# A chunked delta-rule kernel: 32x32 block inverses on VectorE become 16x16, and TensorE does the merging

## The chip, the cores and the metric

One core of one Trainium2 chip runs the whole program. The metric is device microseconds of one execution, the median of several runs. Engine names are short: PE is TensorE's matmul and PEld its weight load, DVE is VectorE, ACT is ScalarE, POOL is GpSimd, SP is SyncE, whose queue here issues almost all DMAs.

## The reference, cut to what matters

The reference is a two-layer backbone over 512 latent and 256 context tokens of width 1024. Layer 0 has window attention beside a bidirectional RWKV-7 mixer, layer 1 a Fourier mixer, and both have a squared-ReLU MLP. The change touches the RWKV scan alone, which the reference writes as a recurrence over tokens, once forward and once backward, for 8 heads of 64:

```python
def step(S, inp):
    r_t, w_t, k_t, v_t, kk_t, a_t = inp
    s_kk = jnp.einsum('bhvk,bhk->bhv', S, kk_t)
    S = (S * w_t[:, :, None, :]
         - s_kk[..., None] * (kk_t * a_t)[:, :, None, :]
         + v_t[..., None] * k_t[:, :, None, :])
    return S, jnp.einsum('bhvk,bhk->bhv', S, r_t)
```

## The kernel before, in words

The kernel takes the tokens in chunks of 64. Within a chunk the recurrence is a triangular system: a 64x64 matrix with ones on its diagonal has to be inverted for each head, chunk and direction. Two chunks make a window of 128 tokens, and there are six windows (two of context, four of latent tokens). So `inverse(i)` inverts, for window `i`, 16 systems in each of two directions. They lie in the tiles `AB[d]` (`ab` in the trace, one of them `sB`), with the rows of a matrix on the partitions.

The work of a window runs through named pieces, which the string `PLAN` (line 1735) lists: `prep` builds decayed keys (`L`, `pgth`, `gq`, `pr`), `mats` makes the matrices on PE and masks them on DVE (`ab`, `ed`), `nat` transposes keys, `inv` is `inverse`, and `u`, `s`, `y` are the serial chain: right-hand side and solution (`zs`, `vu`), the next state (`St`), the output (`y`). `u` of a window needs its inverse and the state that the window before left. Beside them stand the projections (`tile`, dense 128x512 matmuls `ps<-hhi,whi` and the like), attention (`qry`, `max`, `row`, `attn`, with `pT` and `q`), and after them `read` and `out`. Everything behind (both MLPs, the Fourier layer) needs what these give.

`PLAN` is not the order of execution. Every instruction is recorded first (class `Plan`, line 238), and `solve` (line 382) sorts them by engine: a list scheduler with a cost per instruction (`cost`, line 336), a priority from the longest way to the end, buffers as resources, and a guess of TensorE's clock, so that it sets extra matmuls (`warm`, line 646) into gaps that it foresees. `issue` (line 613) then writes the program, so that every instruction shows line 656 and is told apart by its tiles. On each engine the order is fixed: an instruction that waits holds up all behind it.

`inverse` (line 1218) before the change has three parts:

- Gather (lines 1229 to 1250): the 32x32 diagonal blocks go to DRAM (`Dg`) and come back with one block on each of 128 partitions, in the tiles `Minv` and `Mt`. A block takes two partitions, one for each half of 16 rows. Five copies on ACT turn blocks round. `Minv` and `Mt` fill both buffers of the pool tag `p4`.
- VectorE (lines 1252 to 1299): the inverse of each 16x16 half is built by doubling, from 2x2 to 4x4, 8x8 and 16x16, in the tile `Rt`. Then the 16x16 halves are merged to 32x32: four products and four sums over 128x1024 elements (lines 1288 to 1294), with copies on ACT around them, the last a transposition of 64x1024.
- Merging on PE (lines 1301 to 1325): the inverse goes through DRAM (`D2`, `D3`, `D` in the trace) back into `ab` and `Xs`, rows on the partitions. Two groups of 32 small matmuls (32x32 by 32 columns), with an eviction behind each, merge 32x32 blocks to 64x64.

Of the kernel before, what the change touches and what calls it, by code (L numbers as in the profile page):

```python
# [50 lines left out]
def _cst_layout():  # L51
    n = 0
    for name, w in (
        ("ident", 128), ("cent", 128), ("perm", 128), ("mAB", 128), ("mED", 128),
        ("blk", 128), ("hind", 2), ("ones", 1), ("onez", 1), ("sel", 2), ("scan", 512),
        ("cos", T), ("sin", T), ("mS", 384),
    ):
        _CST[name] = (n, n + w)
        n += w
# [6 lines left out]
def _consts():  # L66
# [22 lines left out]
    put("onez", (p > 0)[:, None])  # L89
    put("sel", np.stack([p % 32 == 0, p % 32 == 1], 1))  # L90
# [574 lines left out]
def body(tc, I, out):  # L665
# [547 lines left out]
    I2 = ()  # L1213
    Rt = P.tile([128, 1024], F32, name="Rt")
    pool.memset(Rt, 0.0)
    pool.memset(sub(Rt, 0, [[33, 32]]), 1.0)

    def inverse(i):
        o = O[i]
        ABf = [o.AB[d].rearrange("p c h e t -> p (c h e) t") for d in range(2)]  # L1220
        if i in I2:
            M, Mb, tt = h2("E", name="Minv"), h2("E", name="Mb"), sB
        else:
            Mp, tt = p4((128, 1024), "Minv"), p4((128, 1024), "Mt")
            M, Mb = Mp[:, 0:512], Mp[:, 512:1024]
        Mt = tt
        Dg = dr.tile([2, 2, 16, 1024], F32, tag="Dg", bufs=2, name="Dg")
        rows = lambda u, d: slice(64 * u + 32 * d, 64 * u + 32 * d + 32)
        for d in (1, 0):
            qo = 64 if d == 0 else 0  # L1230
            for b in range(2):
                nc.sync.dma_start(Dg[d, b].rearrange("p (i t) -> i p t", t=32), ABf[d][qo + 32 * b : qo + 32 * b + 32, :, 32 * b : 32 * b + 32])
            Df = Dg[d].rearrange("b p e -> (b p) e")
            for u in range(2):
                if d:
                    nc.sync.dma_start(Mt[rows(u, d), :], Df)
                else:
                    nc.sync.dma_start(M[rows(u, d), :], Df[:, 0:512])
            if d == 0:
                nc.sync.dma_start(Mt[rows(1, 0), 0:496], Df[:, 528:1024])  # L1240
# [4 lines left out]
        by_row, by_col = [[32, 16], [1, 16]], [[1, 16], [32, 16]]  # L1245
        for u in range(2):
            r = rows(u, 1)
            act.copy(part(M, r, 0, by_row), part(Mt, r, 528 * u, by_col))
            act.copy(part(M, r, 16, by_row), part(Mt, r, 512, by_col))
        act.copy(part(M, rows(1, 0), 0, by_row), part(Mt, rows(1, 0), 0, by_row))  # L1250
        R = Rt
# [860 lines left out]
```

## Time and profile before

| | |
|---|---|
| median of 3 runs | 1432.41 us (1432.25 to 1432.7) |
| the profiled execution's own time | 1429.67 us |
| its span, first to last instruction | 1427.9 us |
| PE, DVE, ACT busy over the span | 94%, 60%, 47% |
| mean granted TensorE clock | 0.949 |
| the six inverses, from the first `Dg` issue to the last `D` issue | 202.9 to 504.1 us |

The busy share of PE is not its share of useful work: matmuls are pipelined, their ends are modelled, and at half the granted clock the same matmul is busy for longer. So PE's busy time is read together with the granted clock of the same stretch.

### The profile page before, as it was taken

The numbers are of one execution on the slowest core, as the hardware profiler recorded it, in microseconds if no ns is written. First come the engines' busy times: TensorE is split into PE (matmuls) and PEld (weight loads), VectorE is DVE, ScalarE is ACT, GpSimd is POOL, SyncE is SP. The second block draws the span as 40 slices with busy tenths as digits, with TensorE's granted clock in tenths as the row PEclk, the third lists the DMA queues.
The fourth block names the chain that finished last, engine by engine and source line by source line (L and its number), as shares of the span: only waits on it lengthen the run. The fifth ranks groups of instructions, "written<-read, shape, count | busy, mean of one in ns | idle before, by whom it ended". The sixth has DMA issues, their size and how long they took to land.

```text
span 1427.9 us, 23855 instructions
## 1 busy us (share of the span) xinstructions
PE 1337.8 (94%) x8865; PEld 1083.8 (76%) x8865; DVE 850.9 (60%) x1540; ACT 671.9 (47%) x1331; POOL 328.8 (23%) x352
## 2 busy tenths in 40 slices
PE   6999987788988999999999999999989999999997
PEld 2787875676865776887888888878967888888886
DVE  3844489997585753778655566675976333333334
ACT  3775677664454324446522255332646522255332
POOL 1436476334344233040000000000561000000001
PEclk9999998855799999999999999999999999999999
DMA  9468975736545322335555565562322232323222
GB/s 359 158 214 255 317 230 152 198 97 159 164 132 154 90 71 82 96 89 167 194 178 182 178 193 185 188 211 81 104 59 82 95 97 89 97 95 103 89 89 74
DMA packets 166148, 208.76 MB, mean 146 GB/s; under 512 B 45000, under 2 KB 78792, under 8 KB 166032
## 3 DMA queue, kind: packets, MB, share of 16 engines
q1 hardware_dynamic: 164144, 205.30, 46.8%
q10 hardware_dynamic: 1376, 1.90, 0.4%
q8 instruction: 69, 1.13, 0.3%
q14 instruction: 47, 0.39, 0.1%
q0 software_dynamic: 512, 0.03, 0.0%
HBM read 180.15 MB, written 27.00 MB: 145 GB/s over the span
## 4 chain that ended last, share of the span: by engine, by line
PE 57%; DVE 3%; DMA 1%; issue 1%; ACT 0%; POOL 0%; DVEq 0%; ACTq 0%
PE ps L656 57%; DVE ht L656 1%; DVE wlo L656 1%; DVE fwlo L656 0%; DVE hlo L656 0%; DVE x L656 0%; DMA st<-adaB_in 0%; DMA q<-ml 0%; PE warm L646 0%; DVE wb L656 0%; DVE ulo L656 0%; DVE o L656 0%; DMA st<-wout_in 0%; DVE y L656 0%; DVE sq L656 0%
## 5 line engine op out<-in xcount | busy, mean ns | idle before, releaser
L656 ACT CAST whi<-st 128x512 fp32r<-128x512 f32 x306 | 187.7, 619 | 409.6 <-PE ps L656 370.7
L656 DVE TENSOR_TENSOR wlo<-st,whi 128x512 fp32r<-128x512 f32 x306 | 226.1, 749 | 221.8 <-ACT whi L656 159.8
L656 PE MATMUL ps<-hlo,whi 128*128 128x512 f32 x600 | 230.5, 394 | 4.1 <-DVE hlo L656 4.1
L656 PE MATMUL ps<-hhi,whi 128*128 128x512 f32 x600 | 232.0, 397 | 2.2 <-ACT hhi L656 1.7
L656 PE MATMUL ps<-hhi,wlo 128*128 128x512 f32 x600 | 228.4, 394 | 5.1 <-DVE wlo L656 5.0
L656 PE MATMUL ps<-zhi,whi 128*128 128x512 f32 (+1 forms) x528 | 203.1, 389 | 0.6 <-ACT whi L656 0.6
L656 PE MATMUL ps<-zlo,whi 128*128 128x512 f32 (+1 forms) x528 | 202.2, 389 | 0.0
L656 PE MATMUL ps<-zhi,wlo 128*128 128x512 f32 (+1 forms) x528 | 199.3, 389 | 0.3 <-DVE wlo L656 0.3
L656 PEld LDWEIGHTS ps<-hhi,wlo 128*128 128x128 f32 x600 | 113.0, 189 | 30.4 <-DVE wlo L656 7.0
L656 PEld LDWEIGHTS ps<-hlo,whi 128*128 128x128 f32 x600 | 113.2, 189 | 29.0 <-DVE hlo L656 5.7
L656 PEld LDWEIGHTS ps<-hhi,whi 128*128 128x128 f32 x600 | 112.7, 188 | 27.3 <-ACT hhi L656 2.5
L656 PEld LDWEIGHTS ps<-zhi,whi 128*128 128x128 f32 x528 | 98.8, 188 | 24.0 <-ACT whi L656 1.6
L656 PEld LDWEIGHTS ps<-zhi,wlo 128*128 128x128 f32 x528 | 98.8, 188 | 23.3 <-DVE wlo L656 0.9
L656 PEld LDWEIGHTS ps<-zlo,whi 128*128 128x128 f32 x528 | 98.6, 188 | 22.3
L656 POOL TENSOR_TENSOR rs<-ms,pw 128x4 f32<-128x4 f32 (+1 forms) x7 | 6.2, 885 | 407.4 <-DVE ms L656 407.4
L656 POOL TENSOR_TENSOR wa<-st 128x512 f32<-128x512 f32 x8 | 13.0, 1629 | 342.2 <-DMA st<-fw_in 325.5
L656 POOL TENSOR_TENSOR ada<-ada,sB 128x512 f32<-128x512 f32 x48 | 66.2, 1399 | 42.2 <-DMA ada<-adaB_in 28.6
L656 DVE CUSTOM_DVE_ANT_0 st<-st,sB,vec 128x512 f32<-128x512 f32 x56 | 42.0, 750 | 44.1 <-DMA st<-adaB_in 44.1
L656 PE MATMUL ps<-pr,gq 64*128 64x128 f32 (+1 forms) x384 | 50.0, 341 | 14.7 <-DVE gq L656 11.8
L656 PEld LDWEIGHTS ps<-pr,gq 64*128 64x128 f32 x384 | 44.2, 240 | 20.7 <-issue 13.3
L656 DVE TENSOR_TENSOR zlo<-s,zhi 128x512 fp32r<-128x512 f32 x64 | 44.2, 691 | 25.7 <-ACT zhi L656 25.4
L656 DVE CUSTOM_DVE_ANT_0 st<-st,sB,adv 128x512 f32<-128x512 f32 x56 | 41.9, 749 | 14.2 <-DMA st<-adaB_in 13.6
(390 smaller groups left out, 2579.8 us busy)
## 6 DMA issues: line engine op xcount, KB each, us to landing
st<-w_in SPq DMA_DIRECT2D x256, 256.0 KB, 2.9
st<-adaB_in SPq DMA_DIRECT2D x112, 256.0 KB, 3.1
ada<-adaB_in SPq DMA_DIRECT2D x48, 256.0 KB, 4.9
st<-win_in SPq DMA_DIRECT2D x40, 256.0 KB, 4.5
spl_th<-th SPq DMA_DIRECT2D x16, 384.0 KB, 4.5
pgth<-spl_th SPq DMA_DIRECT2D x24, 256.0 KB, 3.9
st<-adaA_in SPq DMA_DIRECT2D x16, 256.0 KB, 5.1
st<-adaA_in SPq DMA_DIRECT2D x8, 512.0 KB, 6.9
```

Of the source, the lines that this page charges most:

```text
L656: i = getattr(getattr(tc.nc, r.eng), r.op)(*[tr(a) for a in r.args], **{x: tr(a) for x, a in r.kw.items()})
```

## The change

The pieces and `PLAN` stay. In `inverse` VectorE stops at the 16x16 blocks, and a second level of merging on PE comes in.

- Gather: the 16x16 diagonal blocks (four to a matrix) go to DRAM in eight DMAs and come back in two, one block on each partition. One copy on ACT turns the blocks of one direction. All of it lies in one `p4` buffer (`Minv`; the scratch `tt` is a part of it), so two inverses can hold a buffer at a time. `p4` buffers have 768 columns now and had 1024.
- VectorE: the doubling to 16x16 is as before, on 256 elements to a partition (tile `R`). The eight instructions of 128x1024 and the copies around them are gone. One copy on ACT transposes 128x256.
- Way back: `R` and its transposed form go to DRAM in two DMAs, and 16 DMAs of 16 partitions (rows of 64 B) bring them into `ab`, `Yt`, `Vt` and `Xs`. The instruction count on SP goes from 19 DMAs an inverse to 28.
- Merging 16 to 32 on PE: 64 matmuls `ps<-Yt,ab` (32x32 by 16 columns), two evictions with a factor of -1 or 0 to a partition (new constant `zn`) into `Zt`, one on ACT and one on DVE; then 64 matmuls `ps<-Zt,Vt` and 32 `ps<-Vt,Zt`, evicted by two copies on ACT, two on DVE, and two additions into `Xs` on DVE. That makes 160 more matmuls an inverse.
- Merging 32 to 64 stays as it was.
- Setup: `Yt`, `Vt`, `Zt`, `Xs` and `R` are single tiles, cleared or set once on POOL near the start.

The diff, with the removed lines cut:

```diff
+    put("zn", np.where((p % 32 >= 16) == (p >= 64), -1.0, 0.0)[:, None])
...
-    Rt = P.tile([128, 1024], F32, name="Rt")
...
-            Mp, tt = p4((128, 1024), "Minv"), p4((128, 1024), "Mt")
...
-        for step in range(2):
-            ma, a0, a1 = (M, 16, 32) if step == 0 else (Mb, 0, 16)
-            for r0 in (0, 8):
-                dve.tensor_tensor(sub(tt, 0, [[128, 8], [16, 8], [1, 16]]), sub(ma, a0 + a1 * r0, [[a1, 8], [0, 8], [1, 16]]),
-                                  sub(Mb, 256, [[0, 8], [16, 8], [1, 16]]) if step == 0 else sub(pp, 0, [[0, 8], [16, 8], [1, 16]]), ALU.mult)
-                dve.tensor_reduce(sub(pp, r0, [[1, 8], [16, 8]]) if step == 0 else sub(Mb, 384 + 8 * r0, [[8, 8], [1, 8]]),
-                                  sub(tt, 0, [[128, 8], [16, 8], [1, 16]]), AX.X, ALU.add, negate=step == 0)
...
-        act.copy(RT[0:64].rearrange("p (i t) -> p i t", t=32), R[0:64].rearrange("p (i t) -> p t i", t=32))
...
-        nc.sync.dma_start(Xs[64:96], D3[0].rearrange("p i t -> i p t"))
...
+    R = P.tile([128, 256], F32, name="R")
+    pool.memset(R, 0.0)
+    pool.memset(sub(R, 0, [[17, 16]]), 1.0)
+    Yt = P.tile([128, 16, 16], F32, name="Yt")
+    Vt = P.tile([128, 16, 32], F32, name="Vt")
+    Zt = P.tile([128, 16, 32], F32, name="Zt")
+    Xs = P.tile([128, 16, 32], F32, name="Xs")
+    for t in (Yt, Vt, Xs):
+        pool.memset(t, 0.0)
+    for g in range(4):
+        r = slice(32 * g, 32 * g + 32)
+        pool.tensor_copy(Zt[r], ident[r, r].unsqueeze(1).to_broadcast([32, 16, 32]))
     def inverse(i):
         o = O[i]
         ABf = [o.AB[d].rearrange("p c h e t -> p (c h e) t") for d in range(2)]
+        Mw = p4((128, TC), "Minv")
+        M, tt = Mw[:, 0:256], Mw[:, 256:768]
+        Dg = dr.tile([2, 2, 2, 16, 256], F32, tag="Dg", bufs=2, name="Dg")
+        dr_ = [slice(64 * d, 64 * d + 64) for d in range(2)]
+        qo = (64, 0)
+        r16 = lambda d, b, u: slice(qo[d] + 32 * b + 16 * u, qo[d] + 32 * b + 16 * u + 16)
+        r32 = lambda d, b: slice(qo[d] + 32 * b, qo[d] + 32 * b + 32)
         for d in (1, 0):
             for u in range(2):
+                for b in range(2):
+                    c0 = 32 * b + 16 * u
+                    nc.sync.dma_start(Dg[d, u, b].rearrange("s (i t) -> i s t", t=16), ABf[d][r16(d, b, u), :, c0 : c0 + 16])
+            nc.sync.dma_start((tt[64:128, 0:256] if d else M[0:64]), Dg[d].rearrange("u b s e -> (u b s) e"))
+        by_row, by_col = [[16, 16], [1, 16]], [[1, 16], [16, 16]]
+        act.copy(part(M, dr_[1], 0, by_row), part(tt, dr_[1], 0, by_col))
+        full = slice(0, 128)
+        at = lambda t, o, dims: part(t, full, o, dims)
+        dve.tensor_scalar(sub(R, 1, [[34, 8]]), at(M, 1, [[34, 8]]), -1.0, None, ALU.mult)
+        pp = P.tile([128, 64], F32, tag="pp", bufs=1, name="pp")
+        for k in range(2):
+            dve.tensor_tensor(at(tt, 16 * k, [[4, 4], [2, 2], [1, 2]]), at(M, 2 + k, [[68, 4], [16, 2], [0, 2]]), sub(R, 34 + 16 * k, [[68, 4], [0, 2], [1, 2]]), ALU.mult)
+        dve.scalar_tensor_tensor(pp[:, 0:16], tt[:, 0:16], -1.0, tt[:, 16:32], ALU.mult, ALU.subtract)
+        for k in range(2):
+            dve.tensor_tensor(at(tt, 16 * k, [[4, 4], [2, 2], [1, 2]]), sub(R, k, [[68, 4], [16, 2], [0, 2]]), sub(pp, 2 * k, [[4, 4], [0, 2], [1, 2]]), ALU.mult)
+        dve.tensor_tensor(sub(R, 2, [[68, 4], [16, 2], [1, 2]]), at(tt, 0, [[4, 4], [2, 2], [1, 2]]), at(tt, 16, [[4, 4], [2, 2], [1, 2]]), ALU.add)
+        for m in (4, 8):
+            n, s = 8 // m, 34 * m
+            for w in range(n):
+                dve.tensor_tensor(at(tt, m * m * m * w, [[m * m, m], [m, m], [1, m]]), at(M, m + s * w, [[16, m], [0, m], [1, m]]), sub(R, 17 * m + s * w, [[0, m], [1, m], [16, m]]), ALU.mult)
+            dve.tensor_reduce(sub(pp, 0, [[m * m, n], [1, m], [m, m]]), at(tt, 0, [[m * m * m, n], [m * m, m], [m, m], [1, m]]), AX.X, ALU.add, negate=True)
+            for w in range(n):
+                dve.tensor_tensor(at(tt, m * m * m * w, [[m * m, m], [m, m], [1, m]]), sub(R, s * w, [[16, m], [0, m], [1, m]]), sub(pp, m * m * w, [[0, m], [m, m], [1, m]]), ALU.mult)
+            dve.tensor_reduce(sub(R, m, [[s, n], [16, m], [1, m]]), at(tt, 0, [[m * m * m, n], [m * m, m], [m, m], [1, m]]), AX.X, ALU.add)
+        RT = tt[:, 0:256]
+        act.copy(at(tt, 0, by_row), sub(R, 0, by_col))
+        D2 = dr.tile([2, 2, 2, 2, 16, 256], F32, tag="D2", bufs=2, name="D2")
+        nc.sync.dma_start(D2[0].rearrange("d u b s e -> (d u b s) e"), R)
+        nc.sync.dma_start(D2[1].rearrange("d u b s e -> (d u b s) e"), RT)
+        it = lambda t: t.rearrange("s (i t) -> i s t", t=16)
+        for d in (0, 1):
+            fx = d
+            X, XT = D2[1 - d, d], D2[d, d]
+            for b in range(2):
+                c0 = 32 * b + 16 * fx
+                nc.sync.dma_start(Vt[r16(d, b, 1 - fx), :, 16 * (1 - fx) : 16 * (1 - fx) + 16], it(XT[1 - fx, b]))
+                nc.sync.dma_start(ABf[d][r16(d, b, fx), :, c0 : c0 + 16], it(XT[fx, b]))
+                if b == d:
+                    nc.sync.dma_start(Vt[r16(d, b, fx), :, 16 * fx : 16 * fx + 16], it(XT[fx, b]))
+                    nc.sync.dma_start(Xs[r16(d, b, 1 - fx), :, 16 * (1 - fx) : 16 * (1 - fx) + 16], it(X[1 - fx, b]))
+                nc.sync.dma_start(Yt[r16(d, b, fx)], it(X[fx, b]))
+        G = [(d, b, r32(d, b)) for b in range(2) for d in range(2)]
+        hc = lambda d: slice(16 * d, 16 * d + 16)
+        p = pst("iv", (128, 16, 32))
+        for s in range(16):
+            for d, b, r in G:
+                pe.matmul(p[r, s, 0:16], ABf[d][r, s, 32 * b : 32 * b + 32], Yt[r, s, :], start=True, stop=True)
+        act.activation(Zt[64:128, :, hc(0)], p[64:128, :, 0:16], AF.Copy, scale=K("zn")[64:128])
+        dve.tensor_scalar(Zt[0:64, :, hc(1)], p[0:64, :, 0:16], K("zn")[0:64], None, ALU.mult)
+        p = pst("iv", (128, 16, 32))
+        for s in range(16):
+            for d, b, r in G:
+                pe.matmul(p[r, s, 0:16], Zt[r, s, :], Vt[r, s, hc(1 - d)], start=True, stop=True)
+                if b == d:
+                    pe.matmul(p[r, s, 16:32], Vt[r, s, :], Zt[r, s, hc(d)], start=True, stop=True)
+        for d, b, r in G:
+            c0 = 32 * b + 16 * (1 - d)
+            if d == 0:
+                act.copy(ABf[d][r, :, c0 : c0 + 16], p[r, :, 0:16])
+            else:
+                dve.tensor_copy(ABf[d][r, :, c0 : c0 + 16], p[r, :, 0:16])
+            if b == d:
+                dve.tensor_tensor(Xs[r, :, hc(d)], p[r, :, 16:32], Yt[r], ALU.add)
+        Fm = Xs
```

The planner is run on the new instructions and so writes another order. Three places show it; rows are in program order on their engine, `x8` after a row means eight equal instructions.

First DVE, while inverse 0 is on it and `prep` and `mats` of window 2 run beside it (`pgth`, `L` and `gq` of `prep`, `ab` and `ed` of `mats`). Before, from the middle of the merge to 32x32:

```order
L656 TENSOR_TENSOR Mt<-Minv 128x1024
L656 TENSOR_TENSOR ab<-ps,cst 128x4x64
L656 TENSOR_REDUCE pp<-Mt 128x8x8
L656 TENSOR_TENSOR ed<-ps,cst 128x4x64
L656 TENSOR_TENSOR Mt<-Minv,pp 128x1024
L656 SCALAR_TENSOR_TENSOR pgth_2417<-pgth_2542,pgkk 128x512
L656 TENSOR_REDUCE Minv<-Mt 128x64
```

And of the change, the end of the same inverse on DVE:

```order
L657 TENSOR_REDUCE R<-Minv 128x2x4x4
L657 TENSOR_TENSOR Minv<-Minv,R 128x512
L657 TENSOR_REDUCE pp<-Minv 128x8x8
L657 SCALAR_TENSOR_TENSOR pgth_2305<-pgth_2341,pgkk 128x512
L657 TENSOR_TENSOR Minv<-R,pp 128x512
L657 SCALAR_TENSOR_TENSOR L<-cst,pgth_2381 128x512
L657 TENSOR_REDUCE R<-Minv 128x8x8
L657 SCALAR_TENSOR_TENSOR gq<-pgth_2305,L 128x4x64 x2
```

Before, every mask of `mats` and every step of `prep` stands behind an instruction of 128x1024; now the inverse is over with the 128x512 steps, and `gq` of window 2, which PE needs for its next matrices, follows directly.

Second PE, where the first matmuls of inverse 0 stand. Before, all dense projection matmuls are over by then:

```order
L656 MATMUL ps<-hlo,whi 128x512
L656 MATMUL ps<-hhi,wlo 128x512
L656 MATMUL ps<-cst,vc 128x128 x2
L656 MATMUL ps<-cst,vl 128x128 x4
L656 MATMUL ps<-cst,gq 128x128 x8
L656 MATMUL ps<-Xs,ab 32x32 x32
L656 MATMUL ps<-cst,gq 128x128 x8
L656 MATMUL ps<-ab,Xs 32x32
L646 MATMUL warm<-identr 128x512
L656 MATMUL ps<-kst,qst 128x256 x2
```

And of the change, where the first new matmuls stand:

```order
L657 MATMUL ps<-hhi,wlo 128x512
L657 MATMUL ps<-Yt,ab 32x16
L657 MATMUL ps<-hhi,whi 128x512 x2
L657 MATMUL ps<-hlo,whi 128x512
L657 MATMUL ps<-Yt,ab 32x16 x61
L657 MATMUL ps<-qz,cst 128x512
L657 MATMUL ps<-pr,gq 128x128 x8
L657 MATMUL ps<-Vt,Zt 32x16
```

Inverse 0 now comes on PE between the dense matmuls of the last projections (`hhi`, `whi`, `wlo`), and more of these follow between its groups. In the whole program there are 64 `warm` matmuls where there were 97.

Third SP, where inverse 0 leaves VectorE. Before:

```order
L656 DMA Mt<-Dg 32x1024 x2
L656 DMA Mt<-Dg 32x496
L656 DMA D_2656<-Rt 32x1024
L656 DMA D_2658<-Rt 16x1024
L656 DMA D_2656<-Mt 32x1024
L656 DMA D_2658<-Mt 16x1024
L656 DMA st<-win_in 128x512 x2
L656 DMA ab<-D_2656 32x16x32
```

And of the change:

```order
L657 DMA pgk<-spl_k 128x512
L657 DMA Minv<-Dg 64x256
L657 DMA D_2531<-R 128x256
L657 DMA Minv<-Dg 64x256
L657 DMA D_2531<-Minv 128x256
L657 DMA st<-win_in 128x512
L657 DMA ab<-D_2531 16x16x16
L657 DMA Yt<-D_2531 16x16x16
```

In both, loads of inverse 1 (from `Dg`) stand beside the stores of inverse 0. What follows is longer in the change: 16 DMAs of 16 partitions out of `D_2531`, where there were six of 32 partitions.

More of the change, by code (lines that the diff above doesn't have):

```diff
@@ L54, in _cst_layout @@
         ("ident", 128), ("cent", 128), ("perm", 128), ("mAB", 128), ("mED", 128),
-        ("blk", 128), ("hind", 2), ("ones", 1), ("onez", 1), ("sel", 2), ("scan", 512),
+        ("blk", 128), ("hind", 2), ("ones", 1), ("onez", 1), ("zn", 1), ("sel", 2), ("scan", 512),
         ("cos", T), ("sin", T), ("mS", 384),
@@ L1243, in part @@
             return bass.AP(tensor=a.tensor, offset=a.offset, ap=[a.ap[0]] + dims)
[L1245 to L1251, printed above, removed]
-        dve.tensor_scalar(sub(R, 1, [[66, 8]]), sub(M, 1, [[66, 8]]), -1.0, None, ALU.mult)
```

67 lines of the change are left out of this document (removed).

## The prediction, made before the changed kernel ran

> **What bounds the kernel now.** I read the page first, then busy time by stretch, then the waits and the groups of instructions in the stretch that the change touches. From the page, the busy tenths and the granted clock in 40 slices of 35.7 us:
>
> ```profile
> PE   6999987788988999999999999999989999999997
> ...
> DVE  3844489997585753778655566675976333333334
> ...
> PEclk9999998855799999999999999999999999999999
> ```
>
> PE is busy nearly everywhere, but from the sixth to the fourteenth slice DVE is busy too, and there the granted clock falls to half. The inverses lie in these slices. The same in stretches; the columns are the stretch, its length, then busy time and instructions of PE, PEld, DVE, ACT, POOL, the granted clock, DMA:
>
> ```profile
> 0.00:200.00 200.00, 177.75 (x1045) 139.24 (x1046) 112.68 (x178) 125.33 (x279) 93.08 (x90) 0.99 0.79 255
> 200.00:380.00 180.00, 147.47 (x1417) 122.56 (x1416) 152.23 (x283) 112.34 (x248) 81.20 (x111) 0.68 0.58 159
> 380.00:600.00 220.00, 204.65 (x2628) 156.04 (x2627) 133.56 (x315) 91.81 (x195) 76.58 (x86) 0.95 0.38 109
> 600.00:1427.90 827.90, 807.92 (x3785) 666.01 (x3783) 452.38 (x766) 342.39 (x609) 77.91 (x65) 1.00 0.40 127
> ```
>
> I call 200 to 380 us stage A and 380 to 600 stage B; what follows 600 us isn't changed, and I leave its 827.9 us alone. In A, DVE is the busiest engine (152.23 of 180 us) and the clock is 0.68; in B, PE is (204.65 of 220) and DVE has room (133.56). Single stretches of 10 us show how A works:
>
> ```profile
> 240.00:250.00 10.00, 2.14 (x17) 1.71 (x17) 10.00 (x15) 3.59 (x11) 6.58 (x8) 0.61 0.07 27
> 280.00:290.00 10.00, 2.26 (x6) 1.18 (x6) 9.78 (x13) 9.61 (x17) 7.22 (x12) 0.66 0.54 146
> 300.00:310.00 10.00, 9.17 (x96) 8.05 (x96) 9.66 (x21) 6.93 (x19) 1.98 (x3) 0.50 0.21 69
> 310.00:320.00 10.00, 9.63 (x94) 8.32 (x96) 10.00 (x16) 2.80 (x7) 0.00 (x0) 0.50 0.08 28
> 390.00:400.00 10.00, 10.00 (x159) 7.08 (x156) 4.02 (x9) 6.96 (x13) 7.33 (x11) 1.00 0.85 256
> ```
>
> Twice DVE is full while PE stands for nearly 8 us (2.14 and 2.26 us busy); after the second gap the clock is 0.50, and PE is then over 90% busy at half speed. What PE waited for in A, longest first:
>
> ```profile
> PE ps L656 <- DVE gq L656: 11.3, 4, 8.9
> PE ps L656 <- ACT Xs L656: 4.7, 1, 4.7
> PE ps L656 <- DVE Xs L656: 3.5, 1, 3.5
> PE ps L656 <- ACT ab L656: 2.4, 1, 2.4
> PE ps L656 <- ACT gq L656: 2.2, 1, 2.2
> PE ps L656 <- DVE mx L656: 2.0, 1, 2.0
> ```
>
> DVE leads: 11.3 us for `gq` alone, 8.9 of it at once, which is the gap at 240 us, where inverse 0 keeps DVE from the keys of window 2. So A is bound by DVE first, and by a PE at half clock after that; B by PE.
>
> **The change, part by part.** *VectorE gives up the merge to 32x32.* Groups on DVE and ACT between 200 and 600 us, with count, busy time and mean ns:
>
> ```profile
> L656 DVE TENSOR_TENSOR Mt<-Minv 128x1024 f32<-128x1024 f32 x12 | 16.0, 1337 | 0.8 <-ACT Minv L656 0.8
> L656 DVE TENSOR_TENSOR Mt<-Minv,pp 128x1024 f32<-128x1024 f32 x12 | 16.0, 1335 | 0.1
> L656 DVE TENSOR_TENSOR ab<-ps,cst 128x256 f32<-128x256 f32 x39 | 15.6, 413 | 11.3 <-PE ps L656 11.3
> ...
> L656 DVE TENSOR_REDUCE pp<-Mt 128x64 f32<-128x1024 f32 x12 | 14.5, 1205 | 0.0
> L656 DVE TENSOR_REDUCE Minv<-Mt 128x64 f32<-128x1024 f32 x12 | 14.5, 1205 | 0.1
> ...
> L656 DVE COPY zs<-ps 128x256 f32<-128x256 f32 x12 | 5.1, 424 | 16.9 <-PE ps L656 16.8
> ```
>
> Removed are the four groups that write or read 128x1024, 12 instructions each: 16.0 + 16.0 + 14.5 + 14.5 = 61.0 us, 10.2 an inverse. Added are five evictions an inverse (`Zt`, two into `ab`, two additions into `Xs`), all of at most 256 elements to a partition out of PSUM; the nearest rows are 413 and 424 ns, so 5 x 0.42 = 2.1 us. Net 8.1 us less an inverse, 48 in all. Where they lie show the instructions on `Mt`, 24 on DVE for each inverse:
>
> ```profile
> 200.00:380.00 180.00, 66.96 (x96) 19.59 (x24) 0.68 0.58 159
> 380.00:600.00 220.00, 33.10 (x48) 9.85 (x12) 0.95 0.38 109
> ```
>
> 96 of 144 lie in A, four inverses: A loses 32 us of DVE work (152.2 to 120), B 16 (133.6 to 117).
>
> *ACT* loses copies and gains fewer:
>
> ```profile
> L656 ACT COPY Minv<-Mt 32x256 f32<-32x256 f32 x30 | 17.5, 584 | 5.8 <-DMA Mt<-Dg 3.0 <-DMA Minv<-Dg 2.0 <-DMA D<-Mt 0.4
> ...
> L656 ACT COPY Mt<-Rt 64x1024 f32<-64x1024 f32 x6 | 11.9, 1990 | 2.9 <-DVE nm L656 2.6 <-DVE Rt L656 0.2
> ...
> L656 ACT COPY Minv<-Rt 64x128 f32<-64x128 f32 x12 | 4.9, 410 | 10.1 <-DVE Rt L656 10.0
> L656 ACT COPY Minv<-Rt 64x256 f32<-64x256 f32 x12 | 4.8, 404 | 0.2
> L656 ACT COPY zs<-ps 128x256 f32<-128x256 f32 x12 | 4.5, 372 | 7.6 <-PE ps L656 4.7 <-issue 2.8
> ```
>
> These four are 17.5 + 11.9 + 4.9 + 4.8 = 39.1 us, 6.5 an inverse; five copies come, two strided (584 ns by the first row) and three evictions (372 ns by the last), 2.3 us. ACT is at 62% in A and so off the path; I cost the gain at nothing.
>
> *PE gains 160 matmuls an inverse*, 1920 passes in all, since each shows as two instructions (the old groups of 32 give 64). No row has 16 columns. The nearest have 32 (PE, PEld, DVE, ACT, clock, DMA of the tile `Xs` alone):
>
> ```profile
> 424.90:426.13 1.23, 1.20 (x64) 1.09 (x64) 0.00 (x0) 0.00 (x0) 1.00 0.11 40
> ...
> 368.20:370.15 1.95, 1.92 (x64) 1.78 (x64) 0.00 (x0) 0.00 (x0) 0.50 0.58 124
> ```
>
> A pass costs 1.20 / 64 = 18.8 ns at full clock and 1.92 / 64 = 30 at half. With half the columns I bound it by 9.4 and 18.8 at full clock, and take the middle, 14: 4.5 us an inverse, 18 in A and 9 in B. The Trainium skill's page "TensorE: Matmul & The Clock Gate" ("Wait — 56ns, not 53.3ns?") says starts never come closer than about 25 ns however few the columns; by it the new passes would cost 48 us in place of 27. The row above has 18.8 ns at 32 columns, so the trace speaks against that floor here.
>
> *The fillers.* The new order has 64 `warm` matmuls, not 97; 46 lie in A and B now:
>
> ```profile
> 200.00:380.00 180.00, 8.06 (x24) 4.79 (x24) 0.68 0.58 159
> 380.00:600.00 220.00, 7.06 (x22) 3.79 (x22) 0.95 0.38 109
> ```
>
> They fill gaps only, so nothing is gained by itself, and I take their 8.06 and 7.06 us out of PE's work. Cover lost: if gaps return, the clock has less to hold it.
>
> *New waits.* PE now waits twice more in an inverse, for `Zt` and for the second evictions, with the whole of PE's order queued behind. By the waits above a like one cost 4.7 (`ACT Xs`), 3.5 (`DVE Xs`) or nothing; 0 to 5 us each is 0 to 56 us for twelve. In inverses 0 and 1 dense matmuls stand between the groups and hide them. I take about 4 us in A and 3 in B, inside the 95% and 94% of PE's time that the sum below counts as busy.
>
> *DMAs.* An inverse issues 28 in place of 19 on SP:
>
> ```profile
> L656 SPq DMA_DIRECT2D Dg<-ab x22: 319/488/1308, 202.9 to 448.9; - x22
> ```
>
> ```profile
> ab<-D SPq DMA_DIRECT2D x22, 64.0 KB, 3.1
> ```
>
> At 488 ns an issue that is 4.4 us more on SP's queue, with `st`, `edd` and `qd` behind them, and 16 loads in a row end 7.8 us after the first, plus 3.1 us to land. Against that the chain of an inverse loses 10.2 us on DVE and 4 on ACT, and gains 4.5 on PE and two evictions: about 4 us less from end to end. So the bounds are -24 us, if the six chains set the end, and +26, if the new loads stand in the way and nothing covers them. I take 0: dense matmuls cover inverses 0 and 1, and PE sets B. The next inverse no longer waits for two `p4` buffers; I count that as cover, not as gain. The seven setup instructions on POOL come where it is 47% busy (93.08 of 200 us): 0, at most 5 us.
>
> **The sum.** PE's work at full speed is busy time less fillers, by the clock. A: (147.47 - 8.06) x 0.68 = 94.8, and 18 makes 112.8. B: (204.65 - 7.06) x 0.95 = 187.7, and 9 makes 196.7. With 32 us off DVE the two 8 us gaps should close, and the clock falls after them. The clock has two values here, 1.00 and 0.50, so 0.68 means 115 us of A at half. I take 67 of a shorter A: 0.78. This is a choice. Then A lasts 112.8 / (0.78 x 0.95) = 152 us, 28 less, with DVE at 120 of 152. B at 0.97: 196.7 / (0.97 x 0.94) = 215.7, 4 less. Together 32 us less: 1429.67 - 32 = 1397.7 for a profiled execution, and as the median lies 2.7 us above that one (1432.41), 1400.
>
> **The rivals.** *The clock stays up.* If A gets 0.90 and B 1.00, with PE 95% busy, A lasts 132 us (DVE would be 91% busy, the end of what it allows) and B 207: 61 us less, 1371. For it: dense matmuls now lie between the groups of inverses 0 and 1. Against it: at 300 to 320 us the clock stays 0.50 with PE 92% and more busy, so being busy doesn't bring it back while small matmuls run. The same page of the Trainium skill ("What's actually happening") has the clock rise after one busy window of about 3.4 us; by that rule this case would be the likeliest. The trace disagrees for small matmuls: 20 us of them at 0.50.
>
> *PE takes back what DVE gives.* The clock stays at 0.68 and 0.95: A lasts 112.8 / (0.68 x 0.95) = 175 us and B 220: 5 less, 1427. For it: small matmuls make up more of PE's work than before.
>
> *A floor under small passes*, at 25 to 30 ns whatever the clock and columns, 11 to 16 ns above my 14, or 21 to 31 us on PE: A 171 to 180 us, B 223 to 227, so 1427 to 1439. Against it stands 18.8 ns. The lower end is the floor of that page.
>
> *Slower: the clock falls.* The 24 fillers in A and 22 in B go down to about ten, and 960 matmuls on 32x32 of the 128x128 array come in. At 0.62 in A and 0.92 in B, A lasts 191 us and B 227: 19 more, 1451. It decides at 0.66 in A, just under today's 0.68, since 112.8 / (0.66 x 0.95) = 180. For it: the half clock at 300 us. Against it: gaps that DVE made were what the clock fell after.
>
> **How the numbers follow.** Forecast 0.55, the clock stays up 0.19, taken back 0.10, floor 0.06, clock falls 0.10. The forecast's own range is 1385 to 1415 (9.4 to 18.8 ns a pass, 0.75 to 0.85 in A). The range 1371 to 1436 leaves out the lower half of the second case and the last one, 0.2 together. A measurement of this kernel tells 0.2%, 2.9 us, from no change. Faster by more than that: 0.55 + 0.19, 0.07 of the third case and 0.01 of the floor, 0.82. Within it: 0.03 and 0.02 of the same two, 0.05. Slower: 0.10 and 0.03 of the floor, 0.13.
>
> **What would show it.** Right: no instruction of 128x1024 from `Minv`; DVE near 120 us in a stage A of some 152, PE's long waits for `gq` gone, the clock of A near 0.78, 64 passes on `Yt` within 0.6 to 1.2 us at full clock, and the same 828 us after the last `out`. Wrong: A as long as now with PE over 90% busy at 0.68 or less; 64 passes taking 1.6 us or more at full clock; or PE and DVE both idle in A and B with PE waiting for DMAs into `Yt` or `Vt`, which would make the chain of an inverse the bound.

## The result: 12 to 16 us faster, 32 us were forecast

The changed kernel took 1419.76 us (median of 4 runs, 1416.86 to 1421.86) against 1432.56 for the kernel before: a ratio of 0.990, 95% interval 0.988 to 0.993. Measured twice more it took 1418.1 (0.988, 0.984 to 0.993) and 1421.7 us (0.992, 0.989 to 0.995). The forecast was 1400, so some 20 us of the expected 32 are missing. The profiled execution took 1418.5 us, with a span of 1416.7.

The 40 slices of 35.4 us (PE, DVE, granted clock in tenths):

```profile
PE   6999989979888999999999999999989999999997
...
DVE  3844497776876344778655566675976332333334
...
PEclk9999998989987899999999999999999999999999
```

The run of 5s in the clock is gone, and DVE is less full in the seventh to tenth slices. In place of the 5s stand single 8s and a 7, down to the fourteenth slice. To compare stages, I cut the execution where PE has done the same full-speed work, without fillers and without the new passes, as the kernel before had done at 380 and 600 us. Those places are 347.2 and 589.4 us:

```profile
200.00:347.20 147.20, 131.07 (x2351) 106.83 (x2350) 104.76 (x226) 84.70 (x199) 68.90 (x95) 0.86 0.57 156
347.20:589.40 242.20, 222.43 (x3598) 176.15 (x3597) 144.12 (x350) 90.25 (x204) 82.27 (x102) 0.89 0.37 104
```

Stage A is 147.2 us long, 32.8 shorter than before, and stage B 242.2, 22 longer. Work at full speed is busy time by the clock, the loss to half clock is the rest of busy time, and idle is the length less busy time:

| us | A forecast | A measured | B forecast | B measured |
|---|---|---|---|---|
| length | 152 | 147.2 | 215.7 | 242.2 |
| PE's work at full speed | 112.8 | 112.7 | 196.7 | 198.0 |
| lost to half clock | 31.8 | 18.4 | 6.1 | 24.5 |
| PE idle | 7.6 | 16.1 | 12.9 | 19.8 |

PE's work was forecast to within 1.3 us; as the stages are cut at equal old work, that tests only what the new passes and the few fillers cost. The sum is 21.7 us longer than forecast: 15.4 of it is PE idle, 5.0 half clock. What PE waited for between 200 and 600 us (total, times, longest):

```profile
PE ps L657 <- issue: 11.3, 6, 2.9
PE ps L657 <- DVE gq L657: 9.0, 4, 4.9
PE ps L657 <- ACT zs L657: 4.8, 3, 3.4
```

"issue" is a wait with no releaser: 11.3 us in six stops, a row that the kernel before doesn't have at all. The longest of them, in order of time (start, length, instructions, and in brackets the idle time before them):

```profile
281.21 0.21 PE L657 MATMUL ps<-Vt,Zt 32*32 32x16 f32 x2
281.27 0.21 PE L657 MATMUL ps<-Zt,Vt 32*32 32x16 f32 x2
284.35 0.26 PE L657 MATMUL ps<-Vt,Zt 32*32 32x16 f32 x8 [2.86 <-issue]
```

In the middle of the run of small matmuls on `Zt` and `Vt` of inverse 1, with all operands there, PE stops for 2.86 us. The stretches around this stop and around the one of inverse 5:

```profile
278.00:281.40 3.40, 3.40 (x193) 3.10 (x189) 2.97 (x6) 0.68 (x2) 1.33 (x2) 1.00 0.92 262
281.40:284.80 3.40, 0.54 (x39) 0.46 (x36) 1.54 (x3) 2.25 (x5) 0.86 (x2) 1.00 0.91 291
284.80:288.20 3.40, 3.40 (x48) 2.92 (x38) 2.01 (x4) 2.49 (x5) 0.00 (x0) 0.50 0.94 278
...
482.80:486.20 3.40, 1.29 (x116) 1.19 (x111) 0.69 (x1) 0.00 (x0) 1.04 (x1) 1.00 0.83 231
486.20:489.60 3.40, 3.06 (x83) 3.03 (x83) 0.83 (x2) 0.36 (x1) 0.00 (x0) 0.50 0.04 10
489.60:499.80 10.20, 10.20 (x108) 8.32 (x110) 1.96 (x6) 1.55 (x3) 2.31 (x3) 0.50 0.01 2
```

Ahead of the stop PE took 193 + 189 = 382 instructions in 3.4 us; during it the clock is still 1.00, and behind it 0.50, for 3.4 us the first time and 13.6 the second. What fits is that PE stands for its own instructions. The page counts them, and so does the queue that brings them, with packets and MB (the first row is the kernel before, the other two the changed one):

```profile
q8 instruction: 69, 1.13, 0.3%
```

```profile
PE 1339.2 (95%) x10752; PEld 1088.7 (77%) x10752; DVE 816.6 (58%) x1516; ACT 642.1 (45%) x1289; POOL 326.7 (23%) x359
...
q8 instruction: 84, 1.38, 0.4%
```

10752 matmuls and as many weight loads are 21504 instructions, 256 for each of the 84 packets of 16.4 KB; there were 69 packets before. During the stop at 281.5 to 284.3 us exactly one such packet starts:

```profile
q8 instruction: 1, 0.02, 2.4%
```

In four of the other five stops none does, since the packet starts up to 2 us ahead of the stop. But in three profiles of the changed kernel all 18 stops end 2.2 to 3.4 us after the start of a packet of this queue. And no two packets of this execution start less than 3.4 us apart, which is 256 instructions in 3.4 us, where PE took 382 in as much time ahead of the stop. This ties the stops to the feeding of instructions. The Trainium skill's page "Runtime: NRT & Kernel Launch" ("Instruction fetch mechanics") has an engine's instructions come in blocks of 256 and calls the cost of crossing from one to the next mostly hidden. The blocks agree; hidden it is not here, 11.3 us show.

### The profile page after: what moved, and what is told of

It is laid out like the page before. It is cut to its first block, busy times and chain, and to the rows that moved or that the text cites. A ratio compares the mean times of both kernels' runs of the same rounds, so it can differ in the third digit from the quotient of the medians.

```text
span 1416.7 us, 27647 instructions
## 1 busy us (share of the span) xinstructions
PE 1339.2 (95%) x10752; PEld 1088.7 (77%) x10752; DVE 816.6 (58%) x1516; ACT 642.1 (45%) x1289; POOL 326.7 (23%) x359
## 4 chain that ended last, share of the span: by engine, by line
PE 75%; DVE 10%; DMA 5%; issue 3%; ACT 3%; SPq 2%; POOL 1%; DVEq 0%; ACTq 0%; POOLq 0%
PE ps L657 74%; SPq L657 2%; DMA st<-adaA_in 1%; DVE wlo L657 1%; DVE ht L657 1%; DVE gq L657 1%; DMA st<-adaB_in 1%; DMA st<-win_in 1%; DVE Minv L657 1%; DVE wb L657 0%; PE warm L647 0%; DVE ab L657 0%; POOL pgth L657 0%; DVE fwlo L657 0%; DMA st<-fw_in 0%
## 5 line engine op out<-in xcount | busy, mean ns | idle before, releaser
L657 PE MATMUL ps<-pr,gq 64*128 64x128 f32 (+1 forms) x384 | 43.5, 328 | 11.2 <-DVE gq L657 11.2
L657 PEld LDWEIGHTS ps<-pr,gq 64*128 64x128 f32 x384 | 39.1, 228 | 17.5 <-issue 9.2
```

What stands on the lines that cost most here:

```text
L657: i = getattr(getattr(tc.nc, r.eng), r.op)(*[tr(a) for a in r.args], **{x: tr(a) for x, a in r.kw.items()})
```

## The experiments

The theories as they stood: **supply** (runs of small passes outrun the feeding of PE's instructions, PE stops, the clock halves behind it), **chain** (the merges of the late inverses lie bare on PE, which waits for their evictions and loads), **pass** (the new matmuls take more of PE's time than 14 ns each), and later **filler** (the new order has too few dense dummies to hold the clock).

**Half of the windows.** Both inversions stand in one kernel, and a set chooses:

```diff
+    NEW = (0, 1, 2)
...
+    def inverse(i):
...
+        (inverse_new if i in NEW else inverse_old)(i)
```

> The new inversion for windows 0 to 2 only, the old one for windows 3 to 5. Both theories put the gain of the change into the stretch of the first three inverses (VectorE's relief, some 28 us) and its loss behind 350 us, so both expect 1400 to 1410 us here, less than the changed kernel's 1419.8. A theory by which the added passes themselves cost most (PE takes back) expects half of the changed kernel's gain, about 1426.

> The old inversion for windows 0 to 2, the new one for windows 3 to 5: the loss alone. Supply theory (a burst of small passes outruns the feeding of PE's instructions, PE stands 1.2 to 2.9 us and the clock halves after it): three or four such stops, 1435 to 1450 us, slower than before. Chain theory (the merges of the late inverses lie bare and PE waits for their evictions and loads): 1440 to 1455. By the prediction's sum for this part (4 us gained) it would be 1428.

Measured: 1413.7 us (ratio 0.985, 0.981 to 0.990) for windows 0 to 2, and 1436.5 us (1.001, 0.998 to 1.003) for 3 to 5. Stages A and B, first of new_first_three, then of new_last_three. B ends where the unchanged 827.9 us of the rest begin, and A ends at the same old work as above, the new passes (here on the tile `ib`) taken out, to within some 3 us:

```profile
200.00:365.50 165.50, 148.35 (x2391) 123.36 (x2391) 128.87 (x271) 97.14 (x228) 73.66 (x111) 0.74 0.53 148
365.50:582.20 216.70, 206.82 (x2628) 157.06 (x2629) 131.37 (x318) 94.58 (x199) 80.51 (x89) 0.94 0.42 118
```

```profile
200.00:360.60 160.60, 130.87 (x1431) 104.50 (x1429) 130.73 (x242) 100.63 (x226) 73.12 (x102) 0.81 0.58 161
360.60:607.90 247.30, 223.97 (x3596) 177.13 (x3593) 144.50 (x350) 90.99 (x206) 85.98 (x107) 0.88 0.37 101
```

In these two runs stage B takes 216.7 us with the old inversion and 247.3 with the new one: the loss goes with the new inversion in the late windows, and the 4 us of gain that the prediction had there don't show. Both theories lived: the stops were 3.1 us in two against 10.2 in five. One thing spoke against a plain story. In new_last_three stage A fell to 160.6 us although inverses 0 to 2 were the old ones there, so the new order by itself moves work between the stages. And 1413.7 missed the 1400 to 1410 that both expected.

**The passes alone, in the kernel before.** Small matmuls that nobody reads, put into its finished order; once in runs of 64 and 96, once dealt out. They were meant to be 160 for each inverse, but the edit finds their places by a PSUM tag (`iv`) that other groups use too. So there are more of them than the expectations count with, 3200 passes in runs and 3520 dealt out in place of 1920, and a part stands before the first inverse or behind the last:

```diff
+        iv = [k for k in seq if first(k) and self.recs[k].claims[0]["tag"] == ("ps", "iv")]
...
+            for d in range(dummy.get(k, 0)):
+                g = slice(32 * (d % 4), 32 * (d % 4) + 32)
...
+                i = tc.nc.tensor.matmul(q, tr(self.idn[g, g]), tr(self.idn[g, g.start : g.start + 16]), start=True, stop=True)
             i = getattr(getattr(tc.nc, r.eng), r.op)(*[tr(a) for a in r.args], **{x: tr(a) for x, a in r.kw.items()})
```

> The kernel before, in its own order, with 160 matmuls of 32x32x16 added to each inverse that nobody waits for and that wait for nothing new: 64 in one run and 96 in another, each ahead of a dense group. They cost 1920 passes, 27 us of PE at 14 ns, part of it under VectorE's gaps. Supply theory: PE stands 1 to 3 us in most of the twelve runs with no releaser, and the clock halves after some: 15 us or more above the same matmuls dealt out singly, 1455 to 1475. Chain theory and pass theory: as long as the dealt ones within 4 us.

> The same 960 matmuls in the kernel before, one to a few ahead of each dense group between the first and the last inverse. Supply theory: no stop without a releaser; only the passes' own time, 10 to 27 us: 1442 to 1455. Chain theory: as dummy_burst. Pass theory (a small pass costs 25 to 30 ns wherever it stands): 1470 and more, as dummy_burst.

Measured: 1472.3 us (1.025, 1.022 to 1.029) in runs, which lies where supply expected it, but with two thirds more passes than it counted with, and 1579.8 us (1.101, 1.097 to 1.105) dealt out, where supply expected 1442 to 1455. From 200 us to the last `out`, the kernel before, then the runs with the dummies' own row (PE and PEld alone) and their stops, then the dealt ones with the dummies' own row:

```profile
200.00:599.60 399.60, 351.72 (x4039) 278.28 (x4038) 285.39 (x598) 204.15 (x443) 157.78 (x197) 0.83 0.47 132
```

```profile
200.00:637.80 437.80, 389.76 (x5920) 313.98 (x5919) 299.54 (x613) 213.32 (x470) 168.68 (x208) 0.82 0.46 126
200.00:637.80 437.80, 23.13 (x1792) 21.58 (x1792) 0.82 0.46 126
...
PE ps L665 <- issue: 5.3, 4, 2.8
PE ps L668 <- issue: 3.1, 3, 1.8
```

```profile
200.00:717.80 517.80, 492.52 (x6358) 367.90 (x6357) 302.00 (x621) 221.47 (x479) 169.84 (x214) 0.79 0.39 111
200.00:717.80 517.80, 76.66 (x2196) 47.77 (x2196) 0.79 0.39 111
```

In runs the dummies take 23.1 us of PE for 1792 passes, 12.9 ns each, and stops without a releaser appear, 8.4 us in seven between 190 and 640 us, where the kernel before has none. So the stops come with such runs alone, with nobody waiting for them: chain can't explain them. Dealt out there are no stops, but 2196 passes take 76.7 us, 34.9 ns each. By the whole time the price is 39 us for 3200 passes in runs, 12 ns each, and 146.5 us for 3520 dealt out, 42 ns each (over the 1433.3 us of the kernel before on the same chip). That fits a high price for going between tiles of 32x32 and 128x128, which wasn't measured by itself. So this pair doesn't price supply; it shows only where the stops come from.

**The instructions taken away.** In the changed kernel's own order each 16 small matmuls on one pair of tiles become one of 256 columns, repeated to choose PE's time (few_passes once, long_passes twice, equal_passes twice on `Yt` and once on `Zt`):

```diff
-                pe.matmul(p[r, s, 0:16], ABf[d][r, s, 32 * b : 32 * b + 32], Yt[r, s, :], start=True, stop=True)
+                m = pe.matmul(p[r, s, 0:16], ABf[d][r, s, 32 * b : 32 * b + 32], Yt[r, s, :], start=True, stop=True)
+                m.alt = (p[r, :, 0:16], Yt[r], 2) if s == 0 else ()
...
+            if r.alt == ():
+                continue
+            for x in range(r.alt[2] if r.alt else 0):
+                i = tc.nc.tensor.matmul(tr(r.alt[0]), tr(r.args[1]), tr(r.alt[1]), start=True, stop=True)
```

> The changed kernel unaltered, so that a second profile shows what repeats. Supply theory: again five or six stops of PE with no releaser in the runs of 32x32x16 matmuls, 10 to 13 us in all, at the same groups, and half clock right after them; 1417 to 1422. Chain theory: the stops without a releaser are chance and lie elsewhere.

> The changed kernel in its own order, but each run of 64 or 32 matmuls of 16 columns is replaced by 8 or 4 matmuls of 256 columns on the same tiles (20 an inverse in place of 160; the blocks are then multiplied by the first block's matrix only, so that part of the computation is left out). PE's time for them is about as before, the evictions, loads and waits are the same, the instructions are an eighth. Supply theory: no stop without a releaser, the clock falls less often, 12 to 25 us less than the changed kernel: 1395 to 1408. Chain theory and pass theory: the same time within 4 us, 1416 to 1424.

> As long_passes, but each only once: 10 matmuls an inverse, half the time on PE, so nearly all of the 27 us of new passes is gone as well (the same part of the computation is left out). Supply theory: a few us below long_passes, 1388 to 1404. Pass theory: the whole gain comes here and not in long_passes, 1395 to 1405. Chain theory: 1410 to 1420, since PE is not what sets the end of the late inverses.

> As long_passes, but with 14 matmuls of 256 columns an inverse in place of 20, so that PE's work is that of the 160 small matmuls (4.3 us an inverse: the runs before gave 0.3 us for each of 256 columns and 13.5 ns for each small pass). The blocks are multiplied by the first block's matrix only, that part of the computation is left out. Supply theory: no stop without a releaser, 6 to 16 us below the changed kernel, 1403 to 1413. Pass theory: 1416 to 1421.

> equal_passes once more beside one_column on one chip, to see how far its 1401.0 us repeats, since few_passes with less work took 1404.8 and long_passes with more 1414.2. Supply theory: 1398 to 1409. If it is above 1412, the gain without small passes was chance of the clock.

Measured: after_again 1418.1, long_passes 1414.2 (ratio 0.985, 0.981 to 0.989), few_passes 1404.8 (0.978, 0.973 to 0.983), equal_passes 1401.0 (0.978, 0.976 to 0.981) and 1407.7 (0.980, 0.976 to 0.985). The stops repeat in the second and third profile of the changed kernel, at the same six matmuls:

```profile
PE ps L657 <- issue: 12.0, 6, 3.1
```

```profile
PE ps L657 <- issue: 13.3, 6, 3.7
```

In the four profiles with few instructions they are gone but for one of 1.1 us, and q8 brings 71 packets in equal_passes. PE's time on `Yt` and `Zt`, first of the changed kernel, then of equal_passes, then of long_passes:

```profile
200.00:600.00 400.00, 10.33 (x768) 8.99 (x768) 5.04 (x12) 0.00 (x0) 0.88 0.44 123
200.00:600.00 400.00, 17.77 (x1152) 16.28 (x1152) 2.82 (x6) 2.81 (x6) 0.00 (x0) 0.88 0.44 123
```

```profile
200.00:572.10 372.10, 11.03 (x96) 4.75 (x96) 5.04 (x12) 0.00 (x0) 0.89 0.46 128
200.00:572.10 372.10, 8.10 (x72) 2.91 (x72) 2.83 (x6) 2.82 (x6) 0.00 (x0) 0.89 0.46 128
```

```profile
200.00:600.00 400.00, 10.63 (x96) 4.28 (x96) 5.04 (x12) 0.00 (x0) 0.91 0.45 125
200.00:600.00 400.00, 20.52 (x144) 9.03 (x144) 2.83 (x6) 2.82 (x6) 0.00 (x0) 0.91 0.45 125
```

The small passes take 10.3 + 17.8 = 28.1 us, 14.6 ns each. equal_passes was meant to match that and has 19.1 (20.5 in its repeat), long_passes 31.2. So neither is a clean match. A straight line between them, 1404.3 at 19.8 (means of the two) and 1414.2 at 31.2, gives 1411.5 at 28.1 us. The changed kernel's three medians have a mean of 1419.8, 8 us more. The same line from few_passes (15.5 us of PE) to long_passes, against after_again, all on one chip, gives 6. So 6 to 8 us are an estimate of what the number of instructions costs by itself; on that chip the intervals of long_passes and after_again overlap, so it isn't a firm one. It is less than the 11 to 13 us that PE stands, and by it 12 to 14 us of the miss aren't supply. These runs don't clear away the other theories alone: chain and pass expected long_passes at 1416 to 1424, which is missed by 2 us only, and few_passes lies where pass expected it. Chain falls by few_passes (1410 to 1420 expected) and by the idle dummies. Pass falls by the 14.6 ns above. Supply, too, is smaller than the 12 to 25 us that it claimed for long_passes.

**The columns taken away.** The same instructions with one column in place of 16:

```diff
+            if r.alt:
+                r.args = (r.alt[0], r.args[1], r.alt[1])
```

> The changed kernel in its own order with one column in place of 16 in each of the 960 small matmuls (15 of 16 columns of these products are left out; each bank is filled once by a dense matmul before, 12 in all, 2.7 us). The number of PE's instructions is that of the changed kernel, nearly all of the columns are gone. Supply theory (the count of instructions costs): the stops without a releaser stay, 9 us or more in all, and the time with them, 1412 to 1424. Column theory (what equal_passes took away is the time of small columns or tiles): stops gone, 1406 or less.

Measured: 1426.7 us (0.993, 0.990 to 0.996). Two waits between 190 and 610 us, and PE's time on `Zt`, then on `Yt`:

```profile
PE ps L665 <- issue: 9.3, 6, 2.7
...
PE ps L660 <- issue: 1.7, 1, 1.7
```

```profile
200.00:590.00 390.00, 17.25 (x1152) 16.07 (x1152) 2.82 (x6) 2.82 (x6) 0.00 (x0) 0.86 0.44 123
200.00:590.00 390.00, 8.60 (x768) 7.68 (x768) 5.04 (x12) 0.00 (x0) 0.86 0.44 123
```

The stops stay at 11.0 us. 1152 passes on `Zt` take 17.25 us where 16 columns took 17.77, and 768 on `Yt` 8.60 where they took 10.33: together 13.5 ns a pass in place of 14.6. That settles the column theory: a small pass keeps over nine tenths of its price with one column in place of 16, and the stops go with the count of instructions. The 7 us above the changed kernel weren't expected; 2.7 are the 12 dense matmuls by the estimate made before the run, the rest is open.

**Fillers.** Dense dummies of 128x512 put in or taken out, the order otherwise unchanged:

```diff
+            for d in range(fillers.get(k, 0)):
...
+                i = tc.nc.tensor.matmul(q, w, w.unsqueeze(1).to_broadcast([128, 4, 128]), start=True, stop=True)
```

> The changed kernel in its own order with four dense dummy matmuls (128x512) ahead of each of the four runs of small matmuls in inverses 3 to 5, 48 in all, 11 us of PE at full clock. Clock theory (the loss behind 350 us is half clock that a little dense work would prevent): half clock behind 350 us falls from 55 us to under 30 and the time by 3 to 10 us, to 1410 to 1417. Supply theory: the stops stay, since the feeding is late and not the work; the fillers cost what they take where PE didn't wait, 1420 to 1430.

> The kernel before, in its own order, without the 44 dense fillers that stand between 190 and 500 us (the changed kernel has 9 there). Filler theory (the change lost time because its planner put in hardly any fillers, so the clock fell in stage B): 1440 to 1452, 6 us or more slower than before, with more half clock. Otherwise the fillers only sat in gaps: 1428 to 1437, and fewer of them can't explain stage B.

> The changed kernel in its own order with 37 dense fillers ahead of the nine matmuls for which PE waited for another engine in both of its profiles (1 to 5 us each); they fill some 60% of each wait. Clock theory: PE's waits stay and the clock holds through them; half clock between 200 and 590 us falls by 20 us or more, 1404 to 1413. Otherwise 1417 to 1424.

> The changed kernel in its own order with eight dense fillers in the middle of five runs of small matmuls, some 20 matmuls ahead of the place where PE stopped without a releaser in both of its profiles (inverse 5 has no free bank and stays as it is). Supply theory: the instructions come in while the fillers run, those five stops go (inverse 5's 2.4 us stays) and the clock holds: 1408 to 1416. Otherwise 40 x 0.23 us and the changes of tile size come on top: 1424 to 1434.

Measured: fill_late 1421.1 (ratio 0.990, 0.986 to 0.994), no_fillers 1434.4 (ratio 1.001, 1.000 to 1.002), fill_waits 1432.0 (0.997, 0.994 to 1.000), fill_stops 1433.6 (1.000, 0.997 to 1.002). Taking 44 fillers from the kernel before changes nothing, which speaks against their lack as the cause in the changed kernel: the filler theory, which asked for 6 us or more, falls. In fill_stops the stops without a releaser are down to 2.4 us, as supply expected. But its time of 1408 to 1416 is missed, since what replaces the stops costs more than they did. From 200 us to the last `out`, the changed kernel, then fill_waits, then fill_stops with its stops:

```profile
200.00:587.30 387.30, 351.41 (x5938) 281.23 (x5938) 248.30 (x576) 174.95 (x403) 151.17 (x196) 0.88 0.44 124
```

```profile
200.00:604.60 404.60, 377.21 (x5987) 293.72 (x5985) 248.53 (x577) 176.14 (x405) 148.64 (x196) 0.85 0.42 118
```

```profile
200.00:606.90 406.90, 376.48 (x6000) 290.19 (x6000) 244.99 (x578) 175.87 (x405) 149.51 (x197) 0.88 0.42 118
...
PE ps L663 <- issue: 2.4, 4, 1.0
```

PE is busy 377.2 and 376.5 us in place of 351.4, so 37 and 40 fillers cost some 26 and 25 us, over 0.6 us each (in fill_waits a part of that is the lower clock), and the clock, 0.85 and 0.88, didn't rise above the 0.88 it had. In fill_late, where 48 fillers stand ahead of runs and not within them, PE is busy 358.5 us, 7 more than in the changed kernel. So in fill_stops, at the changed kernel's clock, it is the dense matmuls in the middle of small ones that are dear, which fits dummy_spread. In fill_late 11.8 us of stops remain, and the time is that of the changed kernel: the clock theory missed there too. This test is weaker than meant: the fillers were placed by the same tag `iv`, and stand in inverses 1 to 4 (289.6 to 454.4 us) and not in 3 to 5.

**Other mixtures.** The same two-way kernel with other sets, and two repeats on one chip:

> The new inversion for windows 0 and 1 only, where VectorE holds PE back most, the old one for 2 to 5; a version that computes the whole. Supply theory: at most two stops of the six, 3 to 5 us, and VectorE relieved by 16 to 20 us where it was full: 1408 to 1420. If the gain needs all six windows: 1422 to 1430.

> The changed kernel once more, beside the two mixed versions on one chip: 1416 to 1422 by both of its measurements.

> The new inversion for windows 0 to 2 and the old one for 3 to 5, once more (1413.7 before). Supply theory: stage A keeps most of the gain with two stops, stage B is fed as in the kernel before: 1408 to 1417, below the changed kernel by 3 us or more. If the first measurement was chance: 1418 to 1424.

> The new inversion for windows 0 to 3, the old one for 4 and 5. Supply theory: two of the four late stops go, those of inverses 4 and 5, and stage B is between: 1408 to 1420. If only the order of the whole plan decides, anything between 1413 and 1437 (new_first_three and new_first_two), and no theory here foretells it.

Measured: new_first_two 1436.5 (1.001, 0.997 to 1.004), new_first_four 1437.0 (1.002, 1.000 to 1.004), first_three_again 1413.4 (0.986, 0.984 to 0.989) beside the changed kernel's 1421.7. Three windows beat the kernel before by 20 us and the changed one by 6 to 8, where the intervals on one chip touch (0.984 to 0.989 against 0.989 to 0.995); two or four gain nothing. Supply foretold the repeat of three windows, and no theory the other two: new_first_two has one stop of 1.3 us, new_first_four five of 9.2 us, and both are as slow as the kernel before. Their stages A, cut to within some 3 us, are about as long as its 180 us:

```profile
200.00:380.00 180.00, 139.22 (x2035) 115.39 (x2034) 135.97 (x269) 99.02 (x225) 78.14 (x107) 0.74 0.51 140
```

```profile
200.00:378.00 178.00, 139.54 (x2700) 119.09 (x2702) 128.24 (x269) 93.62 (x222) 76.61 (x111) 0.77 0.53 144
```

DVE has 136 and 128 us to do in A there, 16 and 24 less than before, and the time doesn't follow. Each set makes the planner lay out the whole order anew, and the versions lie up to 24 us apart, more than the effects that I wanted to tell apart with them.

## Why the prediction was wrong

**What bounds the kernel:** for stage A the changed kernel fits it, but it isn't shown. A became 32.8 us shorter, where 28 were forecast, and the longest wait for `gq` fell from 8.9 us to 4.9. But all waits for `gq` together fell only from 11.3 to 9.0 us, new_last_three has a stage A of 160.6 us with the old inversion in it, and new_first_two and new_first_four have one of some 180 us with DVE relieved. So the planner's order has a share in A's length that no run here separates from DVE's relief, and that the forecast came near it is in part luck.

**VectorE's relief:** 48 us were forecast; by the two profile pages DVE's busy time fell by 850.9 - 816.6 = 34.3. Summed by instruction it fell by some 50 in the inversion itself, but the operations that make `pgth` and `gq` took 8 us longer in the changed kernel. Of more weight is where the rest went. DVE did 104.8 us in A (120 forecast) and 144.1 in B (117 forecast): in the new order PE is further ahead of DVE at the cut, and A's gain is in part work put off into B.

**The passes:** right. 14 ns were forecast, 14.6 measured, and PE's work was met in both stages. That is luck in part: 14 was the middle of two bounds that scale with the columns, and one_column shows that columns hardly count. The rival of a floor had that right, but the floor lies at 13 to 15 ns and not at 25 to 30, and its 1427 to 1439 us didn't come.

**The step that failed** is the one for waits and clock in the sum: "I take about 4 us in A and 3 in B, inside the 95% and 94% of PE's time that the sum below counts as busy", and for B a clock of 0.97, up from 0.95, for which the prediction gives no row. PE was busy 89% of A and 92% of B, and B's clock was 0.89. The waits that this step counted, for `Zt` and the second evictions, hardly came: in the three profiles of the changed kernel PE waited 0.4 to 0.6 us for `Xs`, and for `Zt` in one of them alone, 0.9 us. I had counted what the passes cost PE, and not that the instructions themselves, 15 packets of 256 more than before, must reach it, and in short runs. The runs showed stops without a releaser, 11.3, 12.0 and 13.3 us in three profiles, absent in the kernel before, present with idle dummies, gone with few instructions, and still there with one column. By the estimate above the instructions' number costs 6 to 8 us of the 20 missing. In each of the three profiles half clock begins at five of the six stops, within the stop or up to 3.4 us behind its end, and the sixth falls into half clock. Whether the stops bring it isn't shown, since half clock comes without them too: equal_passes has a clock of 0.82 in A, the changed kernel 0.86.

**What stays open** are the other 12 to 14 us. By the table A came out 5 us shorter than forecast and B 26 longer, so they lie in B. Without small instructions B's idle time and half clock don't go back to what the kernel before had there (15.4 and 10.2 us by its rows): equal_passes has, in its stages A and B,

```profile
200.00:343.60 143.60, 136.35 (x1497) 103.93 (x1496) 104.08 (x228) 85.72 (x201) 67.93 (x96) 0.82 0.57 160
343.60:572.10 228.50, 207.47 (x2713) 157.84 (x2713) 142.55 (x350) 90.34 (x204) 82.60 (x102) 0.93 0.39 109
```

21.0 us idle and 14.5 lost to half clock in B, with DVE at 142.6 us. That DVE's work was put off into B, so that PE waits for it and the clock falls behind these waits, fits the rows but was only argued: what would hold the clock there (fill_waits) made it slower, and a planner with the old order and the new inversion wasn't tried. DMA issues, the other unknown of the prediction, don't show: PE's waits for `Yt` and `Vt` loads come to 0.8 to 2.0 us in the three profiles.

**The rivals:** "the clock stays up" nearly came true for A (0.86 where it had 0.90) and not for B. "Slower" was to be decided by A's clock, which rose; it was B's that fell. "PE takes back", at 1427, is nearer to the measured time than the forecast, but by another way: it left A's clock at 0.68, and that rose to 0.86.

## What to carry to other kernels

When work moves to TensorE as many tiny matmuls, count the instructions as well as the time: some 380 in 3.4 us is more than was fed here, and PE then stood for one to four microseconds in six of the twelve runs, in each of three profiles. Keep such matmuls in runs all the same, since dealing them out between dense ones cost 42 ns a pass in place of 12. And where a planner lays out the order, compare stages at equal work and not at equal time, because a stage can look faster by leaving its neighbour's work for later; then try the change on a part of its loop too, as three of the six windows here gave 20 us where all six gave 12 to 16. Measure each such part, as two and four windows gave nothing.

## What the runs showed of the hardware that was not expected

- PE's instructions came in packets of 256 (16.4 KB), and PE stopped for 0.8 to 3.7 us in the middle of runs of 32x32x16 fp32 matmuls with every operand there. All 18 stops of three profiles ended 2.2 to 3.4 us after the start of a packet.
- A pass of 32x32 took nearly the same with one column as with 16: 25.9 and 28.1 us for 1920, 13.5 and 14.6 ns each. The Trainium skill's page "TensorE: Matmul & The Clock Gate" ("Wait — 56ns, not 53.3ns?") has such a floor, however few the columns, at about 25 ns. The form agrees; the runs show a lower one.
- Small passes dealt out between dense groups added 42 ns each to the time (3520 passes), in runs 12 (3200 passes).
